# A two-layer hybrid trunk in split float32: the decay's low part, the scaling of attention weights, and the turning of compressed weights

## The chip, the core and the metric

The program runs on one core of a Trainium2 chip, in one launch. Its engines are TensorE (PE in the profile; PEld is its weight load), VectorE (DVE), ScalarE (ACT), GpSimd (POOL) and SyncE (SP, which issues most DMAs here). Each takes its instructions in program order and waits for the others by semaphores. The metric is the device time in microseconds (us) of one execution: 1223.88 is the median of three runs of the kernel before (1223.17 to 1225.0).

## The reference

A trunk of two layers on 512 rows of width 1024, in float32. Layer 0 mixes with gated linear attention (GLA), layer 1 with sparse attention (NSA) over keys and values that all its heads share; both also attend to a memory of 256 rows, and both end with a convolutional FFN. What the change touches is the decay of GLA and the attention weights of NSA:

```python
q, k, v, g, lr, mq = split_cols(xn @ gla_w_in[i], GLA_SIZES)
log_a = jax.nn.log_sigmoid((lr @ gla_w_gate_up[i] + gla_b_gate[i]).astype(jnp.float32)) / GLA_GATE_NORM
...
s_c = jnp.einsum('bgrqd,bgkd->bgrqk', qb, kc).astype(jnp.float32) + common_bias(d_c)
p_c = masked_softmax(s_c, d_c >= 0)
o_c = jnp.einsum('bgrqk,bgkd->bgrqd', p_c, vc.astype(jnp.float32))
...
p_s = masked_softmax(s_s, (d_s >= 0)[:, :, None])
...
p_w = masked_softmax(s_w, mask_w)
...
o = gb[..., 0:1] * o_c + gb[..., 1:2] * o_s + gb[..., 2:3] * o_w
```

`lr` has rank 16. A head of NSA has three branches: compressed (31 keys, the weights p_c), selected and window (up to 512 keys each; with 8 blocks of 64 and a top 16, the selected branch takes all blocks). Each branch is scaled by a gate of its own.

## The kernel before

**Split floats.** Matrices are multiplied in float32r, a 4-byte type. For accuracy a float32 value is held as two such parts: the high part by a copy on ACT (line 301 in `split_to`, 287 for weights), the low part, value less high part, by a subtraction on DVE (lines 302 and 288). A product then takes three matmuls, high by high and the two mixed ones.

**GLA's decay.** `rows()` turns `lr` on TensorE into a bank `pb`; ACT writes its high part to two places of `lrs` (lines 690, 691), DVE the low part (line 694). `decay(c)`, for four blocks of 128 rows, multiplies `lrs` by the gate weights in one matmul (line 699), and ACT takes the absolute value (line 700). These five steps are dealt into the matmuls of the third of four query and key projections, `queries_keys(2)`, by a table `at` from the number of a matmul to a step; the framework that builds the program may put an instruction later than it is written, and the rows further down show what comes out. The first two projections are finished by then, and line 629 takes their results out of their banks with DVE, two instructions for each.

**NSA's steps.** There are 12 steps of 6 half-steps each: for each of six pairs of heads (a, hh = 0 or 1), the query tiles (0, 3), then (1, 2). A step computes scores (`scores`), turns the weights of the step before on TensorE (`weights_t`), adds up values (`values`) and projects later queries (`project`). All matmuls of this stage are chained in written order by `mm` and `tr` (lines 1716 to 1718).

- `scores`: TensorE multiplies keys by the two parts of the queries, Qh and Ql; DVE adds the bias and takes a minimum (line 1787) into P, ACT makes the exponential and its sum (line 1789). When both tiles of a half are done, DVE inverts the sums, and POOL multiplies them by the gates (line 1794) and then P by the result (line 1797), one instruction for each tile over both branches.
- `copies`: SP copies each tile of P into R by one DMA (line 1894), which makes it float32r for the transposes. Three buffers each of P, R and PT.
- `weights_t`: TensorE turns R (line 1718), and DVE or ACT copies the bank to PT (line 1913).
- `compressed(a)`: a generator with four stages. It computes the scores of the compressed branch and its exponentials (line 1818, ACT), masks (line 1820, POOL), sums and inverts (DVE), multiplies the inverse by the gates (line 1825, POOL) and Pc by the result (line 1826, POOL); in its third stage it turns Pc by four float32 transposes, and writes the high part (ACT, line 1831) and the low part (DVE, line 1832) of the turned weights to PcT, of which there are two. `values` multiplies PcT by compressed values that hold their own split.
- `queries(a)`: copies the next pair's queries to qd by DMA and splits them (`split_to`: Qh by ACT, Ql by DVE).

In the loop at the end, the first stage of `compressed(a + 1)` runs in half-step 4 of the pair's second step, the second and third in half-step 0 of the two steps that follow.

PSUM banks go by tag (`sc`, `po`, `acc`, `pt`, two of each): a bank is written again only when the instructions that read it are done.

Of the kernel before, what the change touches and what calls it, by code (L numbers as in the profile page):

```python
# [12 lines left out]
F32 = mybir.dt.float32  # L13
FR = mybir.dt.float32r
AF = mybir.ActivationFunctionType
ALU = mybir.AluOpType
# [166 lines left out]
class Trunk:  # L183
# [374 lines left out]
    def gla_layer(self):  # L558
        nc, I, tc = self.nc, self.I, self.tc
        with ExitStack() as outer:  # L560
# [8 lines left out]
            with tc.tile_pool(name="glap", bufs=1) as pp:  # L569
# [115 lines left out]
                def rows():  # L685

                    pb = self.ps("po")
                    for t in range(4):
                        self.behind(nc.tensor.transpose(pb[:16, 128 * t:128 * t + 128], lrT[:, t], self.ident), self.last)
                    nc.scalar.activation(lrs[:16], pb[:16], AF.Copy)  # L690
                    self.rowed = nc.scalar.activation(lrs[32:48], pb[:16], AF.Copy)
                    for t in range(2, 4):
                        self.behind(value(t), self.rowed)
                    nc.vector.tensor_tensor(out=lrs[64:80], in0=pb[:16], in1=lrs[:16].bitcast(F32), op=ALU.subtract)

                def decay(c):

# [2 lines left out]
                    nc.scalar.activation(la[:, c, :], z[:, :384], AF.Abs)  # L700
                    pz.append(z)

                at = {13 + 3 * c: lambda c=c: decay(c) for c in range(4)}
                at[6] = rows
                at[2] = lambda: self.rms_rows(S, "", self.last, bank)
                third = queries_keys(2, None, at)
# [1 line left out]
                    next(third)  # L708
                rb = self.rb
                for i in range(2):  # L710
                    for _ in queries_keys(i):
                        pass
                for _ in third:
                    pass
# [836 lines left out]
    def nsa_layer(self):  # L1551
        nc, I, tc = self.nc, self.I, self.tc
        with ExitStack() as outer:
# [213 lines left out]
            def scores(s):  # L1767
# [3 lines left out]
                for hh in range(2):  # L1771
# [4 lines left out]
                    for j, qt in enumerate(qts):  # L1776
# [5 lines left out]
                        for brs in ((0, 1),) if qt < 2 else ((0,), (1,)):  # L1782
                            sc = self.ps("po" if brs == (1,) else "sc")
                            for i in range(2):
                                mm(sc[:, :n * len(brs)], Q[i][:, ts], K[g][:, brs[0]:brs[-1] + 1, :n], start=i == 0, stop=i == 1)
                            for br in brs:
                                nc.vector.tensor_tensor_reduce(out=P[:, br, :n], in0=sc[:, n * (br - brs[0]):n * (br - brs[0]) + n], in1=bias, scale=1.0, scalar=3e38,  # L1787
                                                               op0=ALU.add, op1=ALU.min, accum_out=mn[:, br:br + 1])
                                nc.scalar.activation(P[:, br, :n], P[:, br, :n], AF.Exp, scale=-1.0, bias=mn[:, br:br + 1], accum_out=f[:, j, br:br + 1])  # L1789
                            if qt == qts[1] and brs[-1]:  # L1790
                                nc.vector.reciprocal(f, f)
                                gt = bass.AP(tensor=gates.tensor, offset=gates.offset + 36 * qts[0] + 18 * hh + 3 * a + 1,
                                             ap=[gates.ap[0], [36 * (qts[1] - qts[0]), 2], [1, 2]])
                                nc.gpsimd.tensor_tensor(out=f, in0=f, in1=gt, op=ALU.mult)
                                for i, t in enumerate(qts):
                                    P = by_branch(flat[:, spans[qts][i]])
                                    nc.gpsimd.tensor_tensor(out=P, in0=P, in1=f[:, i, :].unsqueeze(2).to_broadcast([128, 2, 128 * t + 128]), op=ALU.mult)  # L1797
                                scaled.append((s, hh, flat))
                            yield

            def compressed(a):
# [23 lines left out]
                nc.gpsimd.tensor_tensor(out=f.rearrange("p (n b) -> p n b", n=4), in0=f.rearrange("p (n b) -> p n b", n=4), in1=g, op=ALU.mult)  # L1825
                nc.gpsimd.tensor_tensor(out=Pv, in0=Pv, in1=f.unsqueeze(2).to_broadcast([128, 8, 32]), op=ALU.mult)
                yield
                pt = self.ps("pt")
                for n in range(4):
                    tr(pt[:64, 128 * (3 - n):128 * (4 - n)], Pc[:, n, :, :], self.ident)  # L1830
                nc.scalar.activation(PcTs[a % 2][:64], pt[:64, :], AF.Copy)
                nc.vector.tensor_tensor(out=PcTs[a % 2][64:], in0=pt[:64, :], in1=PcTs[a % 2][:64].bitcast(F32), op=ALU.subtract)
                yield

            run = lambda g, n=1: [next(g, None) for _ in range(n)]
# [42 lines left out]
            main = [None] * 6 + mo  # L1878
            with tc.tile_pool(name="nsac", bufs=2) as cp:
                o = [self.t(self.tmp, [128, S], tag, bufs=n) for tag, n in (("sqacc", 1), ("sq", 2), ("sq", 2))]  # L1880
                PcTs = [self.t(cp, [128, S], f"PcT{i}", FR, bufs=1) for i in range(2)]

                turned = {}

                def copies():

                    while scaled:
# [2 lines left out]
                        direct = s == 11 and hh == 1  # L1890
                        R = flat if direct else self.t(cp, [128, 1280], "R", FR, bufs=3)
                        for sp, t in zip(spans[qts], qts):
                            if not direct:
                                nc.sync.dma_start(R[:, sp].bitcast(F32), flat[:, sp])
                            Ps[a, t, hh] = by_branch(R[:, sp]), F32 if direct else FR

                def weights_t(s):
# [19 lines left out]
                def values(s):  # L1917

                    a, qts = steps[s]
                    if qts[0] == 0:  # L1920
                        pos[a] = self.ps("po")
                        for i in range(2):
                            mm(pos[a], vcz[a // 3][:, i], PcTs[a % 2], start=i == 0, stop=False, skip_group_check=True)
                    po = pos[a]
                    for qt in qts:
                        ts = slice(128 * qt, 128 * qt + 128)
# [21 lines left out]
                for s, (a, qts) in enumerate(steps):  # L1948
# [6 lines left out]
                    for i in range(6):  # L1955
                        if i == 4:
                            run(before)
                        if a < 5 and i == 4:
# [3 lines left out]
                            else:  # L1962
                                c = compressed(a + 1)
                                run(c)
                        if a < 5 and i == 1 and qts[0]:
                            run(q, 2)
                        run(ahead)
# [39 lines left out]
```

## Time and profile before

| | us |
|---|---|
| median of 3 runs | 1223.88 |
| lowest, highest | 1223.17, 1225.0 |
| the profiled execution, its own time | 1224.9 |
| its span in the profile | 1223.1 |
| busy: TensorE | 1211.6 |
| busy: DVE, ACT, POOL | 912.5, 729.7, 275.2 |
| the four decay products (line 699) start | 36.29 to 38.32 |
| NSA's 12 steps, from the first copies of R on | about 705 to 820 |

The granted clock of TensorE is 0.998 of full speed. A row of the timeline has a start, a duration, the engine, the line of the kernel, the operation and output<-input with their shapes; a bracket at its end says how long the engine stood idle before it, and what released it. The view of waits groups such idle times: the waiting engine, output and line, then what it waited for; in total, times, longest. A stretch of 0 to 9 in the page is the share of the span in tenths.

### The profile page before, as it was taken

How to read it: one execution, taken by the hardware profiler on the slowest of the kernel's cores; microseconds unless marked ns; L12 is line 12 of the kernel's file. 1: busy time of each engine (PE TensorE's matmuls, PEld its weight loads, DVE VectorE, ACT ScalarE, POOL GpSimd, SP SyncE). 2: the span in 40 equal slices, each digit the busy share in tenths (PEclk: the TensorE clock that was granted, in tenths of full speed). 3: DMA queues.
4: the chain of work that ended last, by engine and by line, in shares of the span. 5: the costliest groups of instructions: out<-in, count | busy, mean ns of one | idle time of the engine just before them, and what ended most of it. 6: DMA issues, size and time to landing. Idle time of an engine off the chain costs nothing.

```text
span 1223.1 us, 22059 instructions
## 1 busy us (share of the span) xinstructions
PE 1211.6 (99%) x8321; PEld 1077.9 (88%) x8321; DVE 912.5 (75%) x1637; ACT 729.7 (60%) x1459; POOL 275.2 (23%) x290
## 2 busy tenths in 40 slices
PE   9999999999999999999999999999999999999997
PEld 8887889889999998888888878878899999998887
DVE  7667886698888889644776878875788888889431
ACT  7656655467666667333544677764576666675331
POOL 1000000014444420000003366660034444400000
PEclk9999999999999999999999999999999999999999
DMA  7541113236666652323725467643256666633221
GB/s 262 155 138 60 36 36 104 103 101 171 158 157 156 156 128 86 125 87 109 210 104 172 125 207 234 206 166 121 72 144 163 157 156 156 156 104 108 103 69 69
DMA packets 59776, 163.09 MB, mean 133 GB/s; under 512 B 7309, under 2 KB 13384, under 8 KB 59670
## 3 DMA queue, kind: packets, MB, share of 16 engines
q1 hardware_dynamic: 47638, 140.66, 34.0%
q0 software_dynamic: 10944, 19.93, 10.7%
q8 instruction: 65, 1.06, 0.4%
q10 hardware_dynamic: 1088, 1.10, 0.3%
q14 instruction: 41, 0.34, 0.1%
HBM read 116.13 MB, written 2.15 MB: 97 GB/s over the span
## 4 chain that ended last, share of the span: by engine, by line
PE 94%; DVE 2%; issue 1%; ACT 1%; DMA 1%; POOL 1%; POOLq 0%; DVEq 0%; ACTq 0%
PE pt L1186 18%; PE acc L326 10%; PE po L1186 9%; PE acc L1419 7%; PE acc L1003 6%; PE po L1358 5%; PE sc L1358 5%; PE sc L1186 5%; PE po L346 3%; PE acc L789 3%; PE po L1717 3%; PE acc L1717 2%; PE acc L1482 2%; PE acc L1623 2%; PE acc L346 2%; PE sc L1717 1%
## 5 line engine op out<-in xcount | busy, mean ns | idle before, releaser
L287 ACT ACTIVATE wh<-wraw 128x1024 fp32r<-128x1024 f32 (+1 forms) x105 | 109.4, 1043 | 140.6 <-PE sc L1358 29.6
L288 DVE TENSOR_TENSOR wl<-wraw,wh 128x1024 fp32r<-128x1024 f32 (+1 forms) x105 | 128.7, 1227 | 74.8 <-ACT wh L287 74.0
L1175 DVE TENSOR_TENSOR wl<-wraw,wh 128x1024 fp32r<-128x1024 f32 x76 | 72.6, 955 | 7.0 <-ACT wh L1172 7.0
L326 PE MATMUL acc<-xh,wh 128*128 128x512 f32 x184 | 72.6, 395 | 0.0
L326 PE MATMUL acc<-xl,wh 128*128 128x512 f32 x184 | 71.9, 391 | 0.0
L326 PE MATMUL acc<-xh,wl 128*128 128x512 f32 x184 | 71.9, 391 | 0.0
L1419 PE MATMUL acc<-a,wh 128*128 128x512 f32 x228 | 71.1, 389 | 0.0
L1166 POOL DMA_DIRECT2D wraw<-rbw x38 | 33.4, 879 | 153.3 <-DVE wl L1175 113.9
L1175 DVE TENSOR_TENSOR wl<-rbw,wh 128x1024 fp32r<-128x1024 f32 x38 | 46.5, 1225 | 26.5 <-ACT wh L1172 26.5
L1056 DVE SCALAR_TENSOR_TENSOR hc<-acc,ntap,hc 128x511 f32<-128x511 f32 x76 | 56.9, 749 | 10.0 <-ACT hc L1053 8.0
L1172 ACT ACTIVATE wh<-wraw 128x1024 fp32r<-128x1024 f32 x76 | 63.9, 843 | 0.6 <-DMA wraw<-rbw 0.5
L1797 POOL TENSOR_TENSOR P<-P,ssm 128x256 f32<-128x256 f32 (+3 forms) x48 | 61.8, 1309 | 1.9
L1056 DVE SCALAR_TENSOR_TENSOR hc<-acc,vec,hc 128x511 f32<-128x511 f32 x76 | 56.9, 749 | 3.0 <-ACT hc L1053 1.7
L1789 ACT ACTIVATE P<-P,smn 128x128 f32<-128x128 f32 (+3 forms) x96 | 53.3, 558 | 7.5 <-DVE smn L1787 6.9
L1161 POOL TENSOR_TENSOR rbw<-s,rbw 128x512 f32<-128x512 f32 x36 | 47.8, 1329 | 36.8 <-DVE xh L1064 19.0
L1358 PE MATMUL po<-a,wh 128*128 128x512 f32 x144 | 56.0, 389 | 0.0
L1358 PE MATMUL sc<-a,wh 128*128 128x512 f32 x144 | 56.0, 389 | 0.0
L1172 ACT ACTIVATE wh<-rbw 128x1024 fp32r<-128x1024 f32 x38 | 40.2, 1059 | 23.4 <-issue 20.5
L1419 PEld LDWEIGHTS acc<-a,wh 128*128 128x128 f32 x228 | 42.8, 188 | 8.9
L1155 POOL TENSOR_TENSOR s<-wraw,rbw 128x512 f32<-128x512 f32 x34 | 44.8, 1317 | 21.4 <-DVE wl L1175 21.4
L1172 ACT ACTIVATE wh<-s 128x512 fp32r<-128x512 f32 x38 | 24.0, 632 | 42.1 <-PE pt L1186 42.1
L1419 PE MATMUL acc<-a,wl 128*128 128x512 f32 x114 | 44.3, 389 | 0.0
(726 smaller groups left out, 4338.7 us busy)
## 6 DMA issues: line engine op xcount, KB each, us to landing
wraw<-in_wp SPq DMA_DIRECT2D x156, 512.0 KB, 3.2
rbw<-in_wp SPq DMA_DIRECT2D x38, 512.0 KB, 4.4
rbw<-rbw POOLq DMA_DIRECT2D x38, 256.0 KB, 4.2
wraw<-rbw POOLq DMA_DIRECT2D x38, 256.0 KB, 3.3
R<-P SPq DMA_DIRECT2D x12, 512.0 KB, 3.3
strip<-vecd SPq DMA_DIRECT2D x12, 448.0 KB, 5.6
R<-P SPq DMA_DIRECT2D x11, 384.0 KB, 3.3
qd<-qf SPq DMA_DIRECT2D x24, 128.0 KB, 3.2
```

The lines of the kernel that those rows point to most:

```text
L287: self.made = nc.scalar.activation(wh, raw, AF.Copy)
L288: self.left = nc.vector.tensor_tensor(out=wl, in0=raw, in1=wh.bitcast(F32), op=ALU.subtract)
L326: self.last = self.nc.tensor.matmul(ps[:M, :N], u[:, M * k:M * k + M], x[k][i][:, :N], start=n == 0, stop=n == 23)
L1003: self.nc.tensor.matmul(ps[:, cols], a[:, o], b[:, cols], start=start and i == 0 and k == ks[0], stop=stop and k == 5 and i == 2)
L1056: return [nc.vector.scalar_tensor_tensor(out=c[:, 2 - i:], in0=u[:, :S - 2 + i], scalar=tap(half, j, i, neg), in1=c[:, 2 - i:], op0=ALU.mu ...
L1172: return after("A", nc.scalar.activation(out, x, AF.Copy))
L1175: return after("D", nc.vector.tensor_tensor(out=out, in0=x, in1=hi.bitcast(F32), op=ALU.subtract))
L1186: after("P", nc.tensor.matmul(bank[:, :256], w[:, o], x, start=start and k + i == 0, stop=k == 3 and i == 2, skip_group_check=True))
L1358: after("P", nc.tensor.matmul(first[m], a[:, o], x, start=r + i == 0, stop=r == NJ - 1 and i == 2))
L1419: nc.tensor.matmul(ps, a[:, o], x, start=n == 0, stop=n == 3 * NJ - 1)
L1717: mm = lambda *args, **kw: pe(nc.tensor.matmul(*args, **kw))
L1797: nc.gpsimd.tensor_tensor(out=P, in0=P, in1=f[:, i, :].unsqueeze(2).to_broadcast([128, 2, 128 * t + 128]), op=ALU.mult)
```

## The change

It has three parts.

1. The decay's low part (line 694) is kept as `self.lowed`, and the evacuations of the first two projections (line 629) are ordered behind it. The four decay products move in the table from ahead of matmuls 13, 16, 19 and 22 (of 24, counted from 0) to ahead of 15, 17, 20 and 23.
2. P is scaled by branch for tiles 2 and 3: two POOL instructions of 512 or 384 columns in place of one of 1024 or 768. `copies` sends each branch of these tiles by a DMA of its own, 69 in place of 46.
3. Compressed weights are split ahead of the transposes. A new stage after the scaling writes the high and low part of Pc to X (high by ACT, low by DVE, `split_to`), side by side, and the four transposes, now of X and in float32r, turn both parts at once. One ACT copy takes the bank to PcT; DVE's subtraction there goes, and PcT has one buffer in place of two. The new stage runs in half-step 3 of the pair's first step, the transposes in half-step 0 of the second step (for the pair 0: in half-steps 0 and 3 of the first step).

```diff
--- before.py
+++ after.py
@@ -691,7 +691,7 @@
                     self.rowed = nc.scalar.activation(lrs[32:48], pb[:16], AF.Copy)
                     for t in range(2, 4):
                         self.behind(value(t), self.rowed)
-                    nc.vector.tensor_tensor(out=lrs[64:80], in0=pb[:16], in1=lrs[:16].bitcast(F32), op=ALU.subtract)
+                    self.lowed = nc.vector.tensor_tensor(out=lrs[64:80], in0=pb[:16], in1=lrs[:16].bitcast(F32), op=ALU.subtract)
 
                 def decay(c):
 
@@ -700,7 +700,7 @@
                     nc.scalar.activation(la[:, c, :], z[:, :384], AF.Abs)
                     pz.append(z)
 
-                at = {13 + 3 * c: lambda c=c: decay(c) for c in range(4)}
+                at = {n: lambda c=c: decay(c) for c, n in enumerate((15, 17, 20, 23))}
                 at[6] = rows
                 at[2] = lambda: self.rms_rows(S, "", self.last, bank)
                 third = queries_keys(2, None, at)
@@ -708,7 +708,7 @@
                     next(third)
                 rb = self.rb
                 for i in range(2):
-                    for _ in queries_keys(i):
+                    for _ in queries_keys(i, self.lowed):
                         pass
                 for _ in third:
                     pass
@@ -1794,7 +1794,10 @@
                                 nc.gpsimd.tensor_tensor(out=f, in0=f, in1=gt, op=ALU.mult)
                                 for i, t in enumerate(qts):
                                     P = by_branch(flat[:, spans[qts][i]])
-                                    nc.gpsimd.tensor_tensor(out=P, in0=P, in1=f[:, i, :].unsqueeze(2).to_broadcast([128, 2, 128 * t + 128]), op=ALU.mult)
+                                    for bs in (slice(0, 2),) if t < 2 else (slice(0, 1), slice(1, 2)):
+                                        w = bs.stop - bs.start
+                                        nc.gpsimd.tensor_tensor(out=P[:, bs], in0=P[:, bs], in1=f[:, i, bs].unsqueeze(2).to_broadcast([128, w, 128 * t + 128]),
+                                                                op=ALU.mult)
                                 scaled.append((s, hh, flat))
                             yield
 
@@ -1825,11 +1828,12 @@
                 nc.gpsimd.tensor_tensor(out=f.rearrange("p (n b) -> p n b", n=4), in0=f.rearrange("p (n b) -> p n b", n=4), in1=g, op=ALU.mult)
                 nc.gpsimd.tensor_tensor(out=Pv, in0=Pv, in1=f.unsqueeze(2).to_broadcast([128, 8, 32]), op=ALU.mult)
                 yield
+                self.split_to(X[:, :, 0], X[:, :, 1], Pc.rearrange("p n b k -> p n (b k)"))
+                yield
                 pt = self.ps("pt")
                 for n in range(4):
-                    tr(pt[:64, 128 * (3 - n):128 * (4 - n)], Pc[:, n, :, :], self.ident)
-                nc.scalar.activation(PcTs[a % 2][:64], pt[:64, :], AF.Copy)
-                nc.vector.tensor_tensor(out=PcTs[a % 2][64:], in0=pt[:64, :], in1=PcTs[a % 2][:64].bitcast(F32), op=ALU.subtract)
+                    tr(pt[:, 128 * (3 - n):128 * (4 - n)].bitcast(FR), X[:, n].rearrange("p a b -> p (a b)"), self.identr)
+                nc.scalar.activation(PcT, pt, AF.Copy)
                 yield
 
             run = lambda g, n=1: [next(g, None) for _ in range(n)]
@@ -1878,7 +1882,8 @@
             main = [None] * 6 + mo
             with tc.tile_pool(name="nsac", bufs=2) as cp:
                 o = [self.t(self.tmp, [128, S], tag, bufs=n) for tag, n in (("sqacc", 1), ("sq", 2), ("sq", 2))]
-                PcTs = [self.t(cp, [128, S], f"PcT{i}", FR, bufs=1) for i in range(2)]
+                PcT = self.t(cp, [128, S], "PcT", FR, bufs=1)
+                X = self.t(cp, [128, 4, 2, 64], "Pcs", FR, bufs=1)
 
                 turned = {}
 
@@ -1890,8 +1895,10 @@
                         direct = s == 11 and hh == 1
                         R = flat if direct else self.t(cp, [128, 1280], "R", FR, bufs=3)
                         for sp, t in zip(spans[qts], qts):
-                            if not direct:
-                                nc.sync.dma_start(R[:, sp].bitcast(F32), flat[:, sp])
+                            n = sp.stop - sp.start
+                            for lo in () if direct else (0,) if t < 2 else (0, n // 2):
+                                c = slice(sp.start + lo, sp.start + lo + (n if t < 2 else n // 2))
+                                nc.sync.dma_start(R[:, c].bitcast(F32), flat[:, c])
                             Ps[a, t, hh] = by_branch(R[:, sp]), F32 if direct else FR
 
                 def weights_t(s):
@@ -1920,7 +1927,7 @@
                     if qts[0] == 0:
                         pos[a] = self.ps("po")
                         for i in range(2):
-                            mm(pos[a], vcz[a // 3][:, i], PcTs[a % 2], start=i == 0, stop=False, skip_group_check=True)
+                            mm(pos[a], vcz[a // 3][:, i], PcT, start=i == 0, stop=False, skip_group_check=True)
                     po = pos[a]
                     for qt in qts:
                         ts = slice(128 * qt, 128 * qt + 128)
@@ -1962,6 +1969,8 @@
                             else:
                                 c = compressed(a + 1)
                                 run(c)
+                        if i == 3 and not qts[0]:
+                            run(c)
                         if a < 5 and i == 1 and qts[0]:
                             run(q, 2)
                         run(ahead)
```

How rows stand on the engines: first DVE at the decay. `lr` is `lrs`, `qk` the evacuated queries and keys, `wl` a weight's low part. Before:

```order
L288 TENSOR_TENSOR wl_608<-wraw_605,wh_607 128x1024 [waits DMAHW6_49,Activation_49]
L629 SCALAR_TENSOR_TENSOR qk_135<-acc_143,rb_433 96x4x128 [waits Activation_49]
L694 TENSOR_TENSOR lr_350<-po_439,lr_350 16x512 [waits PE_49,Activation_49]
L629 SCALAR_TENSOR_TENSOR qk_135<-acc_143,rb_433 32x4x128
L629 SCALAR_TENSOR_TENSOR qk_135<-acc_144,rb_433 96x4x128
L629 SCALAR_TENSOR_TENSOR qk_135<-acc_144,rb_433 32x4x128
```

and after the change:

```order
L288 TENSOR_TENSOR wl_608<-wraw_605,wh_607 128x1024 [waits DMAHW6_49,Activation_49]
L694 TENSOR_TENSOR lr_350<-po_439,lr_350 16x512 [waits PE_49,Activation_49]
L629 SCALAR_TENSOR_TENSOR qk_135<-acc_143,rb_433 96x4x128
L629 SCALAR_TENSOR_TENSOR qk_135<-acc_143,rb_433 32x4x128
L629 SCALAR_TENSOR_TENSOR qk_135<-acc_144,rb_433 96x4x128
L629 SCALAR_TENSOR_TENSOR qk_135<-acc_144,rb_433 32x4x128
```

The subtraction stands ahead of the first evacuation. The brackets name the engines that a row waits for. TensorE at the same place (`wg` are the gate weights; the other matmuls are those of the third projection), before:

```order
L326 MATMUL sc_145<-xl_197,wh_423 128x512
L326 MATMUL sc_145<-xh_208,wh_423 128x512
L699 MATMUL po_460<-wg_240,lr_350 128x384 [waits DVE_49]
L699 MATMUL po_466<-wg_240,lr_350 128x384 [waits PE_49]
L326 MATMUL sc_145<-xh_208,wl_424 128x512
L326 MATMUL sc_145<-xl_209,wh_423 128x512
```

and after:

```order
L326 MATMUL sc_145<-xl_197,wh_423 128x512
L699 MATMUL po_462<-wg_240,lr_350 128x384 [waits DVE_49]
L326 MATMUL sc_145<-xh_208,wh_423 128x512
L326 MATMUL sc_145<-xh_208,wl_424 128x512
L699 MATMUL po_467<-wg_240,lr_350 128x384 [waits PE_49]
L326 MATMUL sc_145<-xl_209,wh_423 128x512
```

The first product stands one matmul earlier, the second two behind the first in place of next to it.

Second, ACT in step 2, the second pair's first step. Before: PT are turned weights, P the scores that become weights, `Qh` the high part of the next pair's queries, `sqacc` an output.

```order
L1913 COPY PT_8201<-pt_8202 128x256 [waits PE_49,Activation_49]
L1789 ACTIVATE P_8212,ssm_8211<-P_8212,smn_8213 128x256 [waits DMAHW1_49,DVE_49,DMAHW2_49,Activation_49,Pool_49]
L1789 ACTIVATE P_8212,ssm_8211<-P_8212,smn_8213 128x256 [waits DVE_49]
L1913 COPY PT_8201<-pt_8221 128x512 [waits PE_49]
L301 ACTIVATE Qh_1514_8250<-qd_8140 128x512 [waits DMAHW4_49,DMAHW3_49]
L1936 COPY sqacc_7860<-po_8064 128x512 [waits PE_49]
L1789 ACTIVATE P_8212,ssm_8211<-P_8212,smn_8256 128x384 [waits DVE_49]
```

After the change, from the same copy on (`Pcs` is X):

```order
L1920 COPY PT_8215<-pt_8216 128x256 [waits PE_49,Activation_49]
L301 ACTIVATE Pcs_7866<-Pc_8107 128x4x64 [waits Activation_49,Pool_49]
L1789 ACTIVATE P_8229,ssm_8228<-P_8229,smn_8230 128x256 [waits DMAHW6_49,DMAHW7_49,DMAHW5_49,DVE_49]
L1789 ACTIVATE P_8229,ssm_8228<-P_8229,smn_8230 128x256 [waits DVE_49]
L1920 COPY PT_8215<-pt_8238 128x512 [waits PE_49]
L301 ACTIVATE Qh_1514_8267<-qd_8153 128x512 [waits DMAHW1_49,DMAHW0_49]
L1943 COPY sqacc_7862<-po_8075 128x512 [waits PE_49]
L1789 ACTIVATE P_8229,ssm_8228<-P_8229,smn_8273 128x384 [waits DVE_49]
```

A row that waits for POOL has come in behind the first copy, and all that follow are one place later.

Third, POOL in the same step, around the two instructions that finish Pc (`cf` are the gated inverses, `ssm` those of P). Before:

```order
L1797 TENSOR_TENSOR P_8048<-P_8048,ssm_8047 128x1024
L1825 TENSOR_TENSOR cf_8174<-cf_8174,gates_6454 128x8 [waits DVE_49]
L1826 TENSOR_TENSOR Pc_8096<-Pc_8096,cf_8174 128x256 [waits Pool_49]
L1794 TENSOR_TENSOR ssm_8148<-ssm_8148,gates_6454 128x4 [waits DVE_49]
L1797 TENSOR_TENSOR P_8149<-P_8149,ssm_8148 128x512 [waits DMAHW6_49,DMAHW5_49,Pool_49]
L1797 TENSOR_TENSOR P_8149<-P_8149,ssm_8148 128x768
```

After:

```order
L1799 TENSOR_TENSOR P_8059<-P_8059,ssm_8058 128x512 x2
L1828 TENSOR_TENSOR cf_8187<-cf_8187,gates_6454 128x8 [waits DVE_49]
L1829 TENSOR_TENSOR Pc_8107<-Pc_8107,cf_8187 128x256 [waits Pool_49]
L1794 TENSOR_TENSOR ssm_8161<-ssm_8161,gates_6454 128x4 [waits DVE_49]
L1799 TENSOR_TENSOR P_8162<-P_8162,ssm_8161 128x512 [waits DMAHW1_49,DMAHW2_49,DMAHW0_49,Pool_49]
L1799 TENSOR_TENSOR P_8162<-P_8162,ssm_8161 128x384 x2
```

The scaling of a large tile has become two instructions of half the width, and what makes Pc stands behind them as before.

## The prediction

> **What bounds the kernel now.** I read the page's busy times first, then the chain that ended last, then the view of what TensorE's instructions waited for.
>
> ```profile
> PE 1211.6 (99%) x8321; PEld 1077.9 (88%) x8321; DVE 912.5 (75%) x1637; ACT 729.7 (60%) x1459; POOL 275.2 (23%) x290
> PE 94%; DVE 2%; issue 1%; ACT 1%; DMA 1%; POOL 1%; POOLq 0%; DVEq 0%; ACTq 0%
> PE sc L1717 <- DVE Ql L302: 1.1, 2, 0.8
> PE po L699 <- DVE lr L694: 1.0, 1, 1.0
> PE pt L1718 <- DMA R<-P: 0.8, 2, 0.6
> PE pt L1718 <- ACT PT L1913: 0.8, 1, 0.8
> ```
>
> TensorE is busy for 99% of the span and makes 94% of the chain. The last four rows (us in total, times, longest) are nearly all the waiting that it does once it runs: under 4 us of 1223. So there is little to win, and TensorE has no slack: whatever makes one of its instructions later makes the end later by as much. Each edit is therefore priced by what it does to TensorE's next start. The profiled execution took 1224.9 us (span 1223.1), 0.1% above the median of 1223.88; I work out a difference against the execution and add it to the median. A measurement of this kernel can tell about 0.2%, or 2.5 us, from no change.
>
> **The decay's low part.** A timeline of the stretch, columns start, duration, engine, line, output<-input:
>
> ```profile
> 34.84 0.68 DVE L629 SCALAR_TENSOR_TENSOR qk<-acc,rb 96x512 f32<-96x512 f32 x1
> 34.93 0.39 PE L326 MATMUL sc<-xh,wh 128*128 128x512 f32 x1
> 35.55 0.68 DVE L694 TENSOR_TENSOR lr<-po,lr 16x512 fp32r<-16x512 f32 x1
> 36.27 2.12 DVE L629 SCALAR_TENSOR_TENSOR qk<-acc,rb 32x512 f32<-32x512 f32 x3
> 36.29 0.62 PE L699 MATMUL po<-wg,lr 97*128 97x384 f32 x2 [0.98 <-DVE lr L694]
> ```
>
> The low part stands behind one evacuation on DVE; TensorE comes free some 0.25 us after 34.93 and waits 0.98 us. Moved ahead, the subtract runs at 34.84 and ends at 35.52, 0.71 us sooner. The first decay product also stands one matmul earlier, so TensorE arrives sooner: it waits some 0.6 instead of 0.98. What is late next are the four evacuations: the first three end at 36.27 + 2.12 = 38.39 in both orders, and TensorE, now early, needs a bank that the fourth frees. I take a gain of **0.5 us** (bounds 0, if the bank takes all of it back, and 1.1, the wait and its gap).
>
> **Transposes of the compressed weights.** Four in float32, four of R in float32r, each with the matmul behind it:
>
> ```profile
> 708.95 0.60 PE L1718 MATMUL pt<-ident,Pc 128*64 128x128 f32 x4
> 709.30 0.42 PE L1717 MATMUL sc<-K,Qh 128*128 128x384 f32 x1
> 713.11 0.46 PE L1718 MATMUL acc<-ident,R 128*128 128x128 f32 x4
> 713.41 0.47 PE L1717 MATMUL acc<-xl,wh 128*128 128x512 f32 x1
> ```
>
> By starts, 0.35 us against 0.30. Six sets give 0.3 us; I take **0.1**, as five of the sets come to stand behind a wait (below); bounds 0 and 0.4. [...]
>
> **Scaling and copying by branch.** Groups of POOL in this stage (count | busy, mean ns), and DMAs of R (KB, us to landing):
>
> ```profile
> L1797 POOL TENSOR_TENSOR P<-P,ssm 128x1024 f32<-128x1024 f32 x12 | 23.7, 1975 | 0.0
> L1797 POOL TENSOR_TENSOR P<-P,ssm 128x512 f32<-128x512 f32 x12 | 12.8, 1067 | 0.9
> R<-P SPq DMA_DIRECT2D x12, 512.0 KB, 3.3
> R<-P SPq DMA_DIRECT2D x11, 256.0 KB, 2.9
> ```
>
> Two ops of 512 cost 2134 ns against 1975: 0.16 us more on POOL for each of 24 ops, off TensorE's path. The first half is ready 0.9 us sooner and its smaller DMA lands 0.4 us sooner, 1.3 us in all. That is more than each of these waits:
>
> ```profile
> 714.96 0.28 PE L1717 MATMUL sc<-K,Qh 128*128 128x256 f32 x1
> 715.07 0.28 PE L1717 MATMUL sc<-K,Ql 128*128 128x256 f32 x1
> 715.63 0.51 PE L1718 MATMUL pt<-ident,R 128*128 128x128 f32 x4 [0.28 <-DMA R<-P]
> 756.65 0.28 PE L1717 MATMUL sc<-K,Ql 128*128 128x256 f32 x1
> 757.49 0.52 PE L1718 MATMUL pt<-ident,R 128*128 128x128 f32 x4 [0.56 <-DMA R<-P]
> ```
>
> A 256-column matmul gives way after 0.11 us (714.96 to 715.07), so the two cost 0.45 and 0.73 by starts: **1.2 us** gained (bounds 0, if the second half or the queue is what they wait for, and 1.4). The DMAs go from 46 to 69 on SP; each lands in some 3 us, far shorter than a half-step, and I price the extra issues at nothing. [...]
>
> **The split of the compressed weights.** This is the large term. Before, the four transposes read Pc itself, and ACT touched only their result. Now ACT makes a high part from Pc, in steps 2, 4, 6, 8 and 10 for the weights of the step after. Its row stands behind a copy of turned weights (PT) and ahead of two exponentials, another copy and the high part of the next queries (Qh), as the rows of the change show. Step 2 of before, in that stretch:
>
> ```profile
> 731.31 1.39 DVE L288 TENSOR_TENSOR wl<-wraw,wh 128x1024 fp32r<-128x1024 f32 x1
> 731.41 0.36 ACT L1913 COPY PT<-pt 128x256 f32<-128x256 f32 x1
> 731.57 1.19 POOL L1825 TENSOR_TENSOR cf<-cf,gates 128x8 f32<-128x8 f32 x1
> 732.84 0.62 POOL L1826 TENSOR_TENSOR Pc<-Pc,cf 128x256 f32<-128x256 f32 x1
> 733.12 0.64 ACT L301 ACTIVATE Qh<-qd 128x512 fp32r<-128x512 f32 x1
> 733.79 1.49 DVE L302 TENSOR_TENSOR Ql<-qd,Qh 128x512 fp32r<-128x512 f32 x1 [1.01 <-ACT Qh L301]
> 735.80 0.62 ACT L1789 ACTIVATE P<-P,smn 128x384 f32<-128x384 f32 x1 [1.42 <-DVE smn L1787]
> 736.07 0.29 PE L1717 MATMUL sc<-K,Ql 128*128 128x256 f32 x1
> 739.22 0.50 PE L1718 MATMUL pt<-ident,R 128*128 128x128 f32 x4
> ```
>
> POOL finishes Pc at 732.84 + 0.62 = 733.46. ACT is at the new row at 731.77, when the copy ends, so it stands for 1.7 us, then splits. The split writes 256 columns; ACT's exponential of 248 in this trace is the nearest row:
>
> ```profile
> L1818 ACT ACTIVATE Pc<-Pc x6: 394/412/413, 699.6 to 810.7; 128x248 f32<-128x248 f32 x6
> L1825 POOL TENSOR_TENSOR cf<-cf,gates x6: 206/1189/1191, 702.8 to 814.2; 128x8 f32<-128x8 f32 x6
> ```
>
> (durations in ns, least/median/most). So ACT is held 1.7 + 0.4 = 2.1 us, and Qh ends at 733.76 + 2.1, about 735.9. DVE's Ql, behind it, takes 1.49 us beside POOL's scaling and less when that is over: I take its end at 736.85 instead of 735.28, 1.6 us later. TensorE asks for it at 736.07: **0.8 us** lost at once. Behind Ql on DVE stand the evacuations of scores, behind those ACT's exponentials and copies, and these free the pt bank that the new transposes want some 1.5 us after Ql: another 0.5. The transposes at 739.22 stood 0.25 us for ACT already, so no slack is left there: TensorE is then late by all **1.6 us**.
>
> Steps 4 and 6 repeat it (L1825 takes 1.19 us in most of its six rows). I take 1.6 us for 6. In step 4 the same, with the R wait of 0.73 inside it counted as gained above. In step 8 Ql was late already:
>
> ```profile
> 797.47 1.85 DVE L302 TENSOR_TENSOR Ql<-qd,Qh 128x512 fp32r<-128x512 f32 x1
> 799.38 0.39 PE L1717 MATMUL sc<-K,Ql 128*128 128x256 f32 x1 [0.75 <-DVE Ql L302]
> 813.11 0.62 ACT L1789 ACTIVATE P<-P,smn 128x384 f32<-128x384 f32 x1
> 814.46 0.61 POOL L1826 TENSOR_TENSOR Pc<-Pc,cf 128x256 f32<-128x256 f32 x1
> 818.06 0.54 PE L1718 MATMUL pt<-ident,R 128*128 128x128 f32 x4 [0.81 <-ACT PT L1913]
> ```
>
> There Ql starts at 797.47 for reasons of its own, late enough that TensorE waits for it, and takes 1.85 us beside POOL; the hold may vanish in that or pass in full, so I take 0.9, about the middle of 0 and 1.6. In step 10 no queries follow. ACT comes to the new row at 813.7, behind the exponential, and Pc ends at 815.07: a stand of 1.35, with the split 1.75. TensorE waited for an ACT copy at 818.06 as it was; I take 1.4, a little under the hold. In step 0 Pc is long done. The losses: 1.6 + 1.6 + 1.6 + 0.9 + 1.4 = **7.1 us**. Bounds: 2.4, if only the first stall at Ql counts (0.8 in steps 2, 4 and 6, nothing in 8 and 10), and 10.2, if each step passes on the whole hold (four of 2.1, one of 1.75).
>
> The DVE row of 1.39 us has both inputs in SBUF and covers POOL's 1.19 us; in step 10, with no such row beside it, the same op takes 0.21. [...]
>
> **Sum.** 7.1 - 0.5 - 0.1 - 1.2 = **+5.3 us**: 1230.2 on the execution's 1224.9, 1229.2 on the median.
>
> **Rivals.**
> - *The hold is mostly hidden.* TensorE stalls at Ql, and the banks behind it have slack after all: loss 2.4, gains 1.8, +0.6 us, 1224.5. For it: ACT idles 1.42 us before its next exponential at 735.80, which could take up two thirds of the hold. Against it: TensorE's 0.25 us at 739.22.
> - *ACT is not held*, because POOL's Pc is finished when ACT gets there; the point is an ACT arrival after 733.4 in step 2's clock. Then only the gains stand, 0.5 + 0.1 + 1.2 = 1.8, or 1222.1; with the upper bounds of the three (1.1, 0.4 and 1.4) 2.9, or 1221.0, and faster. Against it: 1.7 us are missing, and POOL has one instruction more ahead of Pc.
> - *It compounds*: the whole hold of 10.2 us less 1.8: 1232.3.
> - *The halves do not end the R waits*, since TensorE waits for the queue and not for the size: the 1.2 us stay, 1230.4. The first landing time after the change decides it.
> [...]
>
> **How the numbers follow.** Chances: forecast 0.42, R waits left 0.1, hidden 0.21, not held 0.16, compounding 0.08, four passes 0.03. Faster by over 0.2% (below 1221.4): the better part of not held, 0.1. Within 0.2% (to 1226.3): hidden, the rest of not held, four passes: 0.3. Slower: the forecast, R waits left and compounding, 0.6. The range, 1222.0 to 1231.5, leaves out that better part of not held and most of the compounded case. The forecast with what it leaves unsure, 1227 to 1231.5, holds a little over half of the chance by itself.
>
> **What would show it.** On ACT an idle time of 1.3 to 1.7 us ahead of the split's high part, put down to POOL's Pc, in five steps; Qh and Ql 1.6 us later after it; waits of TensorE for Ql and for pt banks of about 1.4 us a step. The decay's wait at 0.6 or less, no wait for R at steps 0 and 4. I am wrong if ACT's idle time there is under 0.5 us, or if it is there and TensorE's waits in these steps do not grow.

## The result, and the profile after

The changed kernel takes 1233.95 us, median of five runs (1232.6 to 1235.12), beside 1223.88 (1223.17 to 1225.24): a ratio of 1.0078, 95% interval 1.0066 to 1.0089. It is slower by 10 us where 5.3 were forecast, and the time lies 2.5 us above the range. The profiled execution is the slowest of the five (1235.12, span 1233.3), and that of before (1224.9) lies above its median too, so the two spans, 10.2 us apart, can be set against each other. Of the executions reported below one, of the kernel with the decay and the scaling by branch alone, took 2399 us, about twice the usual time, for a reason that is not known; no ratio holds it.

From the page after, the busy times and the chain:

```profile
PE 1216.3 (99%) x8321; PEld 1079.1 (87%) x8321; DVE 912.8 (74%) x1637; ACT 732.0 (59%) x1465; POOL 278.9 (23%) x314
PE 88%; ACT 3%; issue 2%; DVE 2%; DMA 2%; POOL 2%; SPq 0%; POOLq 0%; DVEq 0%; ACTq 0%
```

And from its view of TensorE's waits (us in total, times, longest):

```profile
PE pt L1718 <- ACT PT L1920: 5.1, 7, 1.7
PE sc L1717 <- DVE Ql L302: 2.3, 3, 0.8
PE po L699 <- DVE lr L694: 0.9, 1, 0.9
```

As many matmuls as before, and the wait for R's DMA has gone; but TensorE now stands 5.1 us for ACT's copies where it stood 0.8. It is also *busy* for 4.7 us more (1216.3 against 1211.6) with the same number of instructions, which no wait explains. Why ACT is late, its own view of waits says in one row:

```profile
ACT Pcs L301 <- POOL Pc L1829: 8.9, 5, 1.9
```

Five times, up to 1.9 us, ACT stands at the split's high part for POOL. Step 2 in the timeline (POOL's, ACT's, DVE's and TensorE's rows):

```profile
733.01 1.19 POOL L1828 TENSOR_TENSOR cf<-cf,gates 128x8 f32<-128x8 f32 x1
734.28 0.62 POOL L1829 TENSOR_TENSOR Pc<-Pc,cf 128x256 f32<-128x256 f32 x1
732.71 0.36 ACT L1920 COPY PT<-pt 128x256 f32<-128x256 f32 x1
734.93 0.42 ACT L301 ACTIVATE Pcs<-Pc 128x256 fp32r<-128x256 f32 x1 [1.87 <-POOL Pc L1829]
736.70 0.63 ACT L301 ACTIVATE Qh<-qd 128x512 fp32r<-128x512 f32 x1
737.37 1.12 DVE L302 TENSOR_TENSOR Ql<-qd,Qh 128x512 fp32r<-128x512 f32 x1 [0.91 <-ACT Qh L301]
738.54 0.39 PE L1717 MATMUL sc<-K,Ql 128*128 128x256 f32 x1 [0.77 <-DVE Ql L302]
740.01 0.54 PE L1718 MATMUL pt<-ident,Pcs 128*128 128x128 f32 x4 [0.26 <-ACT PT L1920]
```

This is the chain of the forecast, link by link: POOL's late Pc, ACT's stand, Qh and Ql behind it, TensorE's two stops. The starts of TensorE's rows in the two timelines give where the 10.2 us arose. Each line is the growth of the distance between after and before from one landmark to the next; the landmarks are the first scores of the compressed branch and, in each odd step, the first matmul of PT by V.

| stretch | measured, us | forecast, us |
|---|---|---|
| up to the first scores of NSA | +0.7 | -0.5 |
| steps 0 and 1 | +0.6 | -0.5 |
| steps 2 and 3 | +1.75 | +1.6 |
| steps 4 and 5 | +0.9 | +0.9 |
| steps 6 and 7 | +1.7 | +1.6 |
| steps 8 and 9 | +2.3 | +0.9 |
| step 10 to the end | +2.3 | +1.4 |

(The forecast's gain of 0.1 for the transposes is left out; its two R waits are put where they stood.) Steps 2 to 7 came out as reckoned, steps 4 and 5 in part by luck (the term by branch, below). Nearly all of the missing 4.9 us lies in the other lines: 1.2 ahead of NSA, 1.1 in steps 0 and 1, 1.4 in steps 8 and 9, 0.9 from step 10 on. The rest of the document is about the stand itself, which is tested first, and about these four lines.

### The profile page after: what moved, and what is told of

Same layout as the page of the kernel before. It is cut to its first block, busy times and chain, and to the rows that moved or that the text cites. A ratio compares the mean times of both kernels' runs of the same rounds, so it can differ in the third digit from the quotient of the medians.

```text
span 1233.3 us, 22185 instructions
## 1 busy us (share of the span) xinstructions
PE 1216.3 (99%) x8321; PEld 1079.1 (87%) x8321; DVE 912.8 (74%) x1637; ACT 732.0 (59%) x1465; POOL 278.9 (23%) x314
## 4 chain that ended last, share of the span: by engine, by line
PE 88%; ACT 3%; issue 2%; DVE 2%; DMA 2%; POOL 2%; SPq 0%; POOLq 0%; DVEq 0%; ACTq 0%
PE pt L1186 18%; PE acc L326 10%; PE po L1186 9%; PE acc L1419 7%; PE acc L1003 6%; PE po L1358 5%; PE sc L1358 5%; PE sc L1186 5%; PE acc L789 3%; PE po L346 2%; PE po L1717 2%; PE acc L1482 2%; PE acc L1623 2%; PE acc L346 2%; PE acc L1717 1%
## 5 line engine op out<-in xcount | busy, mean ns | idle before, releaser
L1799 POOL TENSOR_TENSOR P<-P,ssm 128x512 f32<-128x512 f32 (+2 forms) x72 | 64.9, 929 | 1.9
```

The costliest lines, as they stand in the source:

```text
L1799: nc.gpsimd.tensor_tensor(out=P[:, bs], in0=P[:, bs], in1=f[:, i, bs].unsqueeze(2).to_broadcast([128, w, 128 * t + 128]), op=ALU.mult)
```

## Experiments

Times are medians, each beside runs of the kernel before on the same chip (1224.2 to 1225.2 there). Single executions differ: the profiled ones reached NSA's first scores anywhere from 2.0 us sooner to 0.7 us later than that of before, whatever was changed. So steps are compared from landmark to landmark, and totals by medians.

**Each part alone.** The three parts of the diff, each applied to the kernel before without the others; first the decay's lines:

```diff
-                    nc.vector.tensor_tensor(out=lrs[64:80], ...
+                    self.lowed = nc.vector.tensor_tensor(out=lrs[64:80], ...
-                at = {13 + 3 * c: lambda c=c: decay(c) for c in range(4)}
+                at = {n: lambda c=c: decay(c) for c, n in enumerate((15, 17, 20, 23))}
-                    for _ in queries_keys(i):
+                    for _ in queries_keys(i, self.lowed):
```

> Only the decay's part of the change. Theory H (ACT's hold for POOL's Pc makes the loss): this part has nothing to do with it; within 0.4 us of the kernel before, as the changed kernel's trace shows no gain there (TensorE's wait for the low part is 0.89 in place of 0.98, and it is level again at 40 us). Rival W: the weight that lands 1.0 us later at 60 us in the changed kernel, and costs 0.7, comes from this part: +0.7 us, and the row of ACT at 60 us has an idle time of 3.0 in place of 2.0.

1224.62 us, ratio 1.0001 (0.9993 to 1.001): no gain, no loss. A weight landed late at 60 us in the changed kernel; by the median this part is not why.

The lines of `scores` and `copies`:

```diff
-                                    nc.gpsimd.tensor_tensor(out=P, in0=P, ...
+                                    for bs in (slice(0, 2),) if t < 2 else (slice(0, 1), slice(1, 2)):
...
-                                nc.sync.dma_start(R[:, sp].bitcast(F32), flat[:, sp])
+                                nc.sync.dma_start(R[:, c].bitcast(F32), flat[:, c])
```

> Only the scaling and the copies by branch. Theory H: a gain of 1.2 us (0.45 in step 0 and 0.73 in step 4, the waits for R's DMA, gone), bounds 0 and 1.4. Rival Q: POOL's longer row and 23 more DMAs on SP cost by themselves, so that a part of the 10 us comes from here: +1 to +3 us.

1222.35 us, ratio 0.998 (0.9971 to 0.9988): a gain of 2.3 us. TensorE's waits in NSA are down to two rows:

```profile
PE pt L1718 <- ACT PT L1918: 0.8, 1, 0.8
PE sc L1717 <- DVE Ql L302: 0.4, 2, 0.2
```

The waits for R's DMA are gone, and those for Ql fell from 1.1 to 0.4. The rival is out: more instructions on POOL and SP cost nothing that shows here. What the gain consists of is less sure: the profile of the decay alone, whose NSA is that of before, has no row for R's DMA either, so a single profile does not show that the halves ended these waits.

The lines of `compressed`, with X, the single PcT and the new stage:

```diff
+                self.split_to(X[:, :, 0], X[:, :, 1], Pc.rearrange("p n b k -> p n (b k)"))
+                yield
...
-                    tr(pt[:64, 128 * (3 - n):128 * (4 - n)], Pc[:, n, :, :], self.ident)
+                    tr(pt[:, 128 * (3 - n):128 * (4 - n)].bitcast(FR), ...
...
+                        if i == 3 and not qts[0]:
+                            run(c)
```

> Only the split ahead of the transposes. Theory H: ACT stands 1.5 to 1.9 us for POOL's Pc in steps 2 to 8, 1.3 in step 10, and the time is 9 to 11 us above the kernel before. Rival Q (POOL's and SP's new instructions make much of it): under +7 us. Rival T (the parts multiply: Pc comes later because POOL's scaling by branch takes longer): idle times of ACT 0.15 us shorter, +7 to +8 us.

1234.04 us, ratio 1.0075 (1.0061 to 1.0089), +9.4 us. ACT stands for POOL as in the whole change:

```profile
ACT Pcs L301 <- POOL Pc L1826: 8.2, 5, 1.7
```

The loss is this part's, all of it. Alone the parts make 0 - 2.3 + 9.4 = +7.1 us. The whole change lies 9.3 us above the 1224.66 of these runs and 10.1 above its own; so the gain by branch is hardly seen beside the split.

**The split at another place.** The whole change, with one number altered:

```diff
-                        if i == 3 and not qts[0]:
+                        if i == 4 and not qts[0]:
```

> The whole change, with the split dealt into half-step 4 in place of 3: ACT has it behind Qh in steps 2, 4, 6 and 8, and behind two exponentials more in step 10. All the work of the change is still done. Theory H: ACT comes there about when Pc is done, its idle time ahead of the split falls under 0.4 us, and 6 us or more of the 10 go: 1223 to 1228 us. Rival D: the loss comes from the work itself (one more instruction for ACT, DVE's low part shut out by POOL, a transposed set that reads X): still +6 us or more.

1224.41 us, ratio 0.9999 (0.999 to 1.0008). Every instruction of the change is still there, and 9.5 us are gone; ACT's view of waits in NSA has no row for POOL any more. So the split's work costs little, and its place in ACT's row costs nearly everything.

**The stand alone.** The kernel before, with a copy that is used for nothing, at the place where the split stood; its target is written over before it is read:

```diff
+                if a:
+                    nc.scalar.activation(PcTs[a % 2][:, :256], Pc.rearrange("p n b k -> p n (b k)"), AF.Copy)
+                    yield
...
+                        if a and i == 3 and not qts[0]:
+                            run(c)
```

> The kernel before, with one ACT copy of 128x256 added in half-step 3 of steps 2, 4, 6, 8 and 10, which reads Pc when POOL has finished it and whose result is overwritten unread. Transposes, DVE's work, POOL's and SP's are those of before. Theory H (ACT's stand for POOL is the loss, by itself): ACT idles 1.5 to 1.9 us ahead of it in steps 2 to 8, and the time is 5 to 9 us above before; step 0 loses nothing. Rival D (the loss needs the split's other work too, DVE's low part and the transposes of X): under +4 us.

1230.30 us, ratio 1.0054 (1.004 to 1.0068): +6.1 us by one ACT instruction in each of five steps, whose row of waits is that of the split:

```profile
ACT PcT L1829 <- POOL Pc L1826: 8.2, 5, 1.7
```

The five copies themselves are about 2 us of ACT (0.4 us each), and the profile has one stretch of 3.4 us at a granted clock of 0.50, from 823.09 on, of the kind that the graded holds below are about. Between the landmarks steps 2 to 7 lost 1.4, 0.6 and 1.4 us here, as in the split alone (1.5, 0.6 and 1.4).

**The same place without the stand.** The whole change, its split in half-step 3, but Pc finished by DVE:

```diff
-                nc.gpsimd.tensor_tensor(out=f.rearrange("p (n b) -> p n b", n=4), ...
+                nc.vector.tensor_tensor(out=f.rearrange("p (n b) -> p n b", n=4), ...
-                nc.gpsimd.tensor_tensor(out=Pv, in0=Pv, in1=f.unsqueeze(2)...
+                nc.vector.tensor_tensor(out=Pv, in0=Pv, in1=f.unsqueeze(2)...
```

> The whole change, the split in half-step 3 as there, but the two instructions that finish Pc (its gates and its scaling) go from POOL to DVE, where they stand ahead of the scaling that POOL has still to do. Theory H (it is POOL's lateness that ACT stands for, not the place of the split): ACT's idle time ahead of the split falls from 1.9 us to under 0.7, and 4 us or more of the 10 go: under 1230 us. Rival P (the place itself costs, wait or no wait): 1231 us or more, with ACT's idle time down.

1223.32 us, ratio 0.9989 (0.998 to 0.9998). ACT's stands are 0.4 us at most now:

```profile
ACT Pcs L301 <- DVE Pc L1829: 1.8, 5, 0.4
```

With the place kept and POOL taken out, the loss is gone. It is POOL's lateness that was paid for.

**Holds of several lengths.** In the split's steps 8 and 10 TensorE's matmuls themselves were slower for a while (below). To see what brings that on, the kernel before got ACT copies that nothing needs, at the split's place and in graded numbers; in a second kernel the long ones stand early:

```diff
+                        if a and i == 3 and not qts[0]:
+                            for _ in range(a + 1):
+                                self.behind(nc.scalar.activation(PcTs[a % 2], rb, AF.Copy), turned[True])
```

> The kernel before, with ACT copies of 128x512 that nothing needs at the same place, 2, 3, 4, 5 and 6 of them in steps 2, 4, 6, 8 and 10 (some 1.0, 1.4, 1.9, 2.4 and 2.9 us of ACT). Theory K (TensorE's clock halves for 3.4 us where it stood idle for some 1.6 us or more of the 3.4 us ahead, and each such time costs 1.6 us beside the stand): no halved clock in the steps where TensorE's waits sum to less than 1.3 us, a halved one of 3.4 us behind most steps where they sum to over 1.8. Rival L (the clock dips belong to the late steps, where DMA and all engines are busiest, or to chance): dips without regard to the waits, or none.

1233.44 us, ratio 1.007 (1.0056 to 1.0084). The holds were better hidden than expected: TensorE's waits in steps 2 to 8 stayed under 1.2 us in any 3.4, and no stretch there was slow. In step 10 it stood 2.75 us in 3.4, and behind it the granted clock was 0.50 for some 3.4 us, from 824.93 on. One event at the latest place does not part the theories, so the order was turned round:

```diff
-                            for _ in range(a + 1):
+                            for _ in range((0, 9, 7, 5, 3, 1)[a]):
```

> As the graded holds, but the long ones early: 9, 7, 5, 3 and 1 ACT copies of 128x512 in steps 2, 4, 6, 8 and 10. Theory K (the clock halves for 3.4 us behind a stretch of 3.4 us in which TensorE stood idle for some 1.5 us or more): halved stretches in steps 2 and 4, where TensorE's idle time should reach 2 us or more, none in steps 8 and 10. Rival L (the late steps are what halves it): none in steps 2 and 4.

1231.41 us, ratio 1.0053 (1.0038 to 1.0069). Windows of TensorE in step 2 (window, its length, PE busy, instructions, granted clock, DMA share, GB/s):

```profile
736.20:739.60 3.40, 1.90 (x12) 1.00 0.70 235
740.00:743.20 3.20, 3.20 (x14) 0.50 1.01 387
744.00:747.20 3.20, 3.20 (x44) 1.00 0.05 18
```

A stretch of 3.4 us with 1.5 us idle, then 3.4 us at a granted clock of 0.50, then 1.00 again. The same happened in step 4, behind 1.7 us idle, and not in steps 6 to 10. Theory K held here, and the late steps were no cause of their own.

**The first pair's set.** The split in half-step 4, and for the first pair made ahead of step 0, so that its transposes stand where they stood before:

```diff
                         if i == 3:
                             run(c)
+                        if i == 7:
+                            run(c)
```

> The whole change with the split in half-step 4, and for the first pair the split made ahead of step 0, so that its transposes stand in half-step 0 as before. Theory B (in step 0 the set of transposes, moved behind the first turned weights, makes the next ones wait for a bank that ACT has not emptied; some 1 us): TensorE's wait of about 1 us for PT in step 0 is gone, and the time is 0.7 to 1.3 us under the kernel with the split in half-step 4 (1224.4), 1223.1 to 1223.7. Rival S (step 0 loses because of the split's work, wherever it stands): no gain.

1224.07 us, ratio 0.9998 (0.9989 to 1.0006). Each against its own runs of before, this kernel is 0.1 us faster and the one without this line 0.25: the medians don't tell the two apart, and the 0.7 us that were expected don't show in them. The timelines do differ. From the first scores to step 1's sums this kernel gains 0.8 us on before, where the other lost 0.2. The wait in step 0 is gone:

```profile
709.32 0.46 PE L1718 MATMUL pt<-ident,Pcs 128*128 128x128 f32 x4
709.62 0.41 PE L1717 MATMUL sc<-K,Qh 128*128 128x384 f32 x1
```

These rows also answer the price of a transposed set: 0.30 us by starts, where four float32 ones took 0.35.

**Combinations.** Without the split, that is the first two parts together; then the two repairs together; then the second part with Pc finished by DVE:

> The change without its split ahead of the transposes. If the parts add up: the sum of the two alone, 2 to 2.5 us under before (1222 us). Rival T (the two parts get in each other's way): within 1 us of before.

1222.64 us, ratio 0.9984 (0.9975 to 0.9993): the parts add up within what can be told.

> The whole change with its split in half-step 3, Pc finished by DVE, and the first pair's split made ahead of step 0. If the two repairs add up (1.4 us in step 0 by the traces, beside the 10 us of the stand): TensorE waits for PT in step 0 no more, and the time is 1221.5 to 1223 us against the 1224.5 of before on this chip, as low as the scaling and copies by branch alone. If not: 1223.3, as with DVE alone.

1221.95 us, ratio 0.9978 (0.9969 to 0.9987): 2.7 us below before, and 12 below the median of the changed kernel. In NSA ACT stands 0.4 us at most for Pc, and no stretch is slow.

> Only the scaling and copies by branch, with Pc finished by DVE and turned by the old float32 transposes. If finishing Pc on DVE has a gain of its own (POOL's next scaling starts some 1.9 us sooner, so R comes sooner and POOL shuts DVE's Ql out for less): 1221 to 1222 us. If it has none: as the part alone, 2 us under before.

1223.07 us, ratio 0.9984 (0.9975 to 0.9993): no gain of its own from DVE beyond the scaling and copying by branch. The intervals of this kernel, the one ahead of it and the second part alone overlap; which of them is best stays open.

## Why the prediction was right in kind and wrong in size

**The bound and the main term were right.** TensorE had no slack, and one ACT instruction that waits for POOL carried through Qh, Ql and the banks to the end. The forecast put ACT's idle time at 1.3 to 1.7 us in five steps; it is 1.8 on average (8.9 in five). It put step 2's stops at 0.8 us for Ql and 0.5 for the pt bank; the rows above show 0.77 and 0.26, by starts 1.0 and 0.4. The stand alone costs 6.1 us; it was priced at 7.1, inside its interval (4.9 to 8.3). That agreement is partly luck: steps 2 to 7 lost 3.4 us with the stand alone, where the forecast has 1.6 for each of the three stands, and the half clock, which it did not reckon with, helped to make up for it.

**What failed, by size:**

1. *"There 0.9" and "I take 1.4", steps 8 and 10.* Measured 2.3 each. The waits were there, but they were priced as idle time alone. What followed them was not idle. Step 8 in the timeline:

```profile
803.82 0.37 PE L1718 MATMUL pt<-ident,R 128*128 128x128 f32 x2 [1.71 <-ACT PT L1920]
805.02 0.63 PE L1003 MATMUL acc<-mo0h,wh 128*128 128x512 f32 x1
808.87 0.40 PE L1003 MATMUL acc<-mo1l,wh 128*128 128x512 f32 x1
```

   and in windows (window, length, PE busy, instructions, granted clock, DMA share, GB/s):

```profile
801.00:804.40 3.40, 1.69 (x12) 1.00 0.60 167
804.60:807.60 3.00, 3.00 (x10) 0.50 0.80 267
808.00:811.40 3.40, 3.40 (x25) 1.00 0.57 199
```

   A matmul of 512 columns takes 0.63 us at 805 and 0.40 at 809; in 3.0 us TensorE does 10 instructions, later 25 in 3.4. The granted clock is 0.50. By this, half the clock for some 3.4 us leaves about 1.7 us of work undone, an estimate; there are two such stretches, in steps 8 and 10 (804.49 to 807.91 and 828.38 to 831.80). The split alone shows what step 8 costs without one. TensorE stopped there for nearly as long, and the clock stayed whole (a timeline row, then windows):

```profile
801.95 0.36 PE L1718 MATMUL pt<-ident,R 128*128 128x128 f32 x2 [1.56 <-ACT PT L1915]
798.60:802.00 3.40, 1.83 (x19) 1.00 0.74 231
802.20:805.40 3.20, 3.20 (x22) 1.00 0.66 226
```

   Between the landmarks steps 8 and 9 lost 0.6 us there, and about 1 with the stand alone, whose clock stayed whole in step 8 as well. So the forecast's 0.9 fits the waits, and the step that failed is that it took a wait to cost its idle time and no more. Of the 4.7 us of busy time that grew without a wait, steps 8 to 11 and what follows hold 2.8. Steps 2 to 7 hold 1.8 at full clock: there matmuls beside a stop last longer (0.39 us for the one of Ql above, 0.29 before). How often the clock fell in the other four executions is not recorded; their mean granted clock, 0.995 to 0.998 beside the 0.998 to 1.0 of before, says that it fell in some.

2. *"In step 0 Pc is long done"*, priced at nothing, with a gain of 0.45 for R. Measured +0.6. The split's wait was indeed none, but its transposes moved behind the first turned weights, and with them the turn of the two pt banks:

```profile
711.89 0.54 PE L1718 MATMUL pt<-ident,Pcs 128*128 128x128 f32 x4
713.96 0.53 PE L1718 MATMUL pt<-ident,R 128*128 128x128 f32 x4 [0.99 <-ACT PT L1920]
713.56 0.35 ACT L1920 COPY PT<-pt 128x256 f32<-128x256 f32 x1
```

   R's next set now needs the bank of the set before it, which ACT copies only at 713.56, behind two exponentials. By branch alone this step gained 0.8 us, so the moved set cost 1.4. Putting it back in place won the 0.8 again in the timeline, though not in the median.

3. *"Moved ahead, the subtract runs at 34.84 and ends at 35.52"*, a gain of 0.5. Measured nothing: the changed kernel is 0.04 us ahead at 33 us and 0.04 ahead at 40, and the part alone gains nothing. The subtract had a second thing to wait for, which the timeline of before showed as plainly, ACT's other high part. First before, then after (two rows):

```profile
34.62 0.59 ACT L691 ACTIVATE lr<-po 16x512 fp32r<-16x512 f32 x1
```

```profile
35.20 0.68 DVE L694 TENSOR_TENSOR lr<-po,lr 16x512 fp32r<-16x512 f32 x1 [0.31 <-ACT lr L691]
35.93 0.45 PE L699 MATMUL po<-wg,lr 97*128 97x384 f32 x1 [0.89 <-DVE lr L694]
```

   It starts when that ends, at 35.2, so it came 0.35 sooner, not 0.71; the products stand a matmul earlier, which eats most of that. Besides, the wait of 0.98 us is not there in every execution: the profiles of the scaling by branch and the stand, each alone and with the decay's lines as before, have no row for it, and that of the graded holds has 0.5 us.

4. *What the sum left to chance.* The profiled execution lost 0.7 us ahead of NSA to a weight that landed 1.0 us later; first before, then after:

```profile
59.40 1.06 ACT L287 ACTIVATE wh<-wraw 128x1024 fp32r<-128x1024 f32 x1 [2.02 <-DMA wraw<-in_wp]
```

```profile
60.40 1.06 ACT L287 ACTIVATE wh<-wraw 128x1024 fp32r<-128x1024 f32 x1 [3.04 <-DMA wraw<-in_wp]
```

   The same instructions stand ahead of it in both, and the decay alone, which has all of the change up to there, costs nothing by the median. I take it as scatter of single executions; that was not shown, and what makes it late was not tried.

**The term by branch** had the right sign, and was too small when alone: 2.3 us in place of 1.2. Beside the waits for R, those for Ql shrank by 0.7. In the profile of before Ql lasts 0.69 us on DVE where none of POOL's scalings runs beside it, and 1.23 to 1.85 us where it starts within one; in the changed kernel it lasts 0.92 to 1.12 us there. That POOL's shorter instructions hold DVE up for less is the author's guess from these rows, and was not tested by itself. In the whole change the term is not there to subtract: the split alone costs 9.4 us, the whole 9.3 to 10.1. In steps 4 and 5 the sum came out at 0.9 as 1.6 for the stand less 0.73 for R's wait; but the split alone, with R copied as before, lost only 0.6 there and has no wait for R, so the halves did not make that difference. Whether TensorE's later start took the wait in, or it was missing by chance, stays open.

**The rivals.** That the whole hold compounds to 1232.3 came nearest, and for another reason than it gave: steps 2 to 7 passed on less than their hold (1.87 + 0.42 us in step 2), and the clock made up the rest. That the hold is hidden and that POOL is done in time are out. The forecast's chances also count four passes for float32 transposes: no run shows such a term, and by starts a float32 set of four took 0.35 us, one of X in float32r 0.30. That the halves do not end the waits for R is not settled: the halves land sooner (2.6 us against 3.3 by the two pages), but the waits are missing without them too.

## What to carry to other kernels

Ask of an instruction that is moved onto an in-order engine not only what it costs but when its input is ready, and what stands behind it: here one 0.4 us copy in each of five steps, placed 1.7 us ahead of its input, cost the kernel 6 us, and the whole split, one half-step later, nothing that could be told. Where the bound engine gets such waits, price the clock too: behind seven of nine stretches of 3.4 us that held some 1.5 us or more of them it was 0.50 for about 3.4 us. And where a set of transposes moves, follow the banks: which earlier set must now be emptied first, and by which engine.

## What the runs showed of the hardware that was not expected

The granted clock of TensorE fell to 0.50 behind waits in the middle of a busy kernel. In the profiles of these runs, in NSA's steps, nine stretches of 3.4 us held some 1.5 us or more of idle TensorE. Behind seven of them the granted clock was 0.50 for about 3.4 us (3.42 both times in the changed kernel): two each in the changed kernel and the reversed holds, one each in the split alone, the stand alone and the graded holds. In the 3.4 us ahead of the slice of 0.2 us in which it fell TensorE was idle for 1.48, 1.49, 1.50, 1.65, 1.68, 1.71 and 2.40 us. Behind two, of 1.56 us each (step 8 of the split alone and of the stand alone), it stayed at 1.00. Behind some twenty stretches that held between 0.75 and 1.16 us it never fell. So the amount alone doesn't decide it.

It is not DMA alone either, whose busy share in the 3.4 us ahead of the seven falls was anything from 0.21 to 0.83, and in the two stretches without a fall 0.68 and 0.66. What else decides stays open.
